# Turning attention probabilities by two row halves of the matrix engine, in a fused hybrid decoder layer

## The chip, the cores and the metric

The kernel runs on one core of one Trainium2 chip. The metric is the device time of one execution in microseconds, as the median of several runs. A core has a matrix engine (PE, whose weight loads the profile lists as PEld), a vector engine (DVE), an activation engine (ACT), a general engine (POOL) and an engine that issues most transfers (SP). They run their own instruction queues in order and meet at semaphores. PE writes into eight PSUM banks of 128 partitions by 512 floats; DVE and ACT copy from there.

## The reference

One decoder layer over 1024 tokens of width 1024. After an RMS norm, one input projection feeds two mixers: four heads of gated DeltaNet and eight heads of dilated sliding-window attention. Their outputs go through one output projection and a residual; a gated MLP with a short convolution and a final norm follow. The part that matters here is the attention: three branches, (window, dilation) of (128, 1), (512, 4) and (2048, 16), joined by their softmax denominators:

```python
for window, dil in DIL_PATTERNS:
    ...
    num, den, m = band_attention(stride(qf), stride(kf), stride(vf), window // dil)
...
out = num_tot / den_tot[..., None]
```

## The kernel before

All work is in one program, `hybrid_layer`. A planner written in the kernel (`Weave`) holds streams of work as generators. Each stream yields the time for which it has to wait by the planner's own costs; the planner then lets the stream with the lowest level run that is due. So PE's instruction order is a weave: the attention stream (level 5) goes when it is due, and between its steps stand the products of the dense projection (level 9) or the output projection (level 8). A dense column is two banks ("hf") of 24 full products each, three for each of eight slices of the input (high and low parts, `mm3`), 512 columns wide. PE's order is stamped and kept; the order on DVE and ACT is chosen by a scheduler, with the operations called through `uv` and `ua` preferred.

The attention works on four head pairs (pi), in each on eight blocks of 128 queries (n), two blocks at a time. A block's two heads (e) lie in partitions 0 to 63 and 64 to 127. In a block the three branches become one softmax over 128 or 256 local keys and up to 192 far keys of the same class mod 4 (`far`), with masks that hold the logarithm of how often a key is counted. The steps for a pair of blocks, each on lines named in the code below:

- `scores` (L900): products of q and k on PE's row halves, into two banks "asc" for the first block and two "atr" for the second. `normalise` (L932) makes probabilities `sm` (queries on partitions, both heads side by side) with DVE, ACT, DVE.
- `turn` (L964): PE turns `sm` so that keys lie on partitions. For each block and head, 128x128 transposes by the identity (`tp`, L192) fill one bank: first the local keys (one or two transposes), then the far ones (up to two). In all 184. `turned` (L945) copies the local part to `pt` with DVE and each far part to `pb` with ACT (L957 to L959).
- `values` (L979) multiplies `pt` with the values, on column halves of the array, one for each head. After four blocks, `merge_classes` (L988) does the same for `pb` ("class products"), and `give` (L1002) copies the result `oT` out of the bank with DVE.

`advance` (L1017) sets the order: turn the pair before, then the scores of the next pair, then the values of the pair before. `turn` yields ahead of each of its four banks, so dense products come between the first block's transposes and the second's. `TSLACK` (L39) shifts these due times.

At the end of the stage three other streams meet the attention. The gates (`gate`, L470: `zz` on ACT and DVE, then `og`) finish the DeltaNet heads. `mixer_splits` (L1067) splits the mixers' outputs into `ohi` and `olo`. `out_proj` (L1095) begins once the last group of blocks has started; its weights `whi` and `wlo` are made by ACT and DVE. The last copy of `turned` is an anchor there: the first low weights, and the slow gate and split operations, are ordered after it (L948 to L955). The scaled copy `xr` (L525) empties the dense banks that the output projection takes over.

Of the kernel before, what the change touches and what calls it, by code (L numbers as in the profile page):

```python
# [9 lines left out]
AF = mybir.ActivationFunctionType  # L10
# [5 lines left out]
P = 128  # L16
# [16 lines left out]
TOKEN = "pe"  # L33
# [5 lines left out]
TSLACK = -1.0, -0.6  # L39
# [105 lines left out]
def hybrid_layer(tc, I, out):  # L145
    nc = tc.nc
    wv = Weave()
# [3 lines left out]
    uv = Engine(wv, nc.vector, "vector", 0.07, 0.00105, first=tc.high_priority)  # L151
    ua = Engine(wv, nc.scalar, "scalar", 0.12, 0.00085, first=tc.high_priority)
    po_ = Engine(wv, nc.gpsimd, "gpsimd", 0.15, 0.0021)
# [9 lines left out]
    def tile_(pool, shape, dt, name, tag, bufs):  # L163
        return wv.slot(pool.tile(list(shape), dt, name=name, tag=tag, bufs=bufs), tag, bufs)
# [3 lines left out]
    def A(name, tag, dt=F32, shape=(P, 1024)):  # L168
        if tag in TURNS:
            i = turns[tag] = turns.get(tag, -1) + 1  # L170
            tag = TURNS[tag][i % len(TURNS[tag])]
        return tile_(lp, shape, dt, name, tag, SLOTS[tag])
# [4 lines left out]
    def const(name, shape, src=None):  # L177
        t = cp.tile(list(shape), F32, name=name)
        if src is not None:
            sy.dma_start(t, src)  # L180
        return t
# [3 lines left out]
    def after(inst, anchor, reason="keeps a slot free until it is needed"):  # L185
        tc.add_manual_dep(inst.ins, anchor.ins.name, order, reason=reason)
# [5 lines left out]
    def tp(dst, src):  # L192
        tc.stamp_issue_order_token(nc.tensor.transpose(dst, src, ident).ins, TOKEN)  # L193
        wv.product(0.11, dst, src)

    def mm3(dst, lhs, rhs, first, last, **kw):
        us = 0.2135 * rhs[0].shape[-1] / 512
        mm(dst, lhs[0], rhs[0], us, first, False, **kw)
        mm(dst, lhs[0], rhs[1], us, False, False, **kw)
        mm(dst, lhs[1], rhs[0], us, False, last, **kw)  # L200
# [23 lines left out]
    n1 = const("n1", [P, KT], I["n1"])  # L224
# [20 lines left out]
    def bank(tag, name="ps"):  # L245
        return tile_(pp_, (P, 512), F32, name, tag, 2)
# [7 lines left out]
    def half(i):  # L254
        return slice(i * 512, i * 512 + 512)
# [63 lines left out]
    ident = const("ident", [P, P], I["ident"])  # L319
# [565 lines left out]
    HALVES = (slice(0, 64), slice(64, 128))  # L885
# [3 lines left out]
    def attention():  # L889
# [52 lines left out]
                div = uv.tensor_scalar(sm[:, e, :wd], sm[:, e, :wd], den[:, e:e + 1], None, op0=OP.mult)  # L942
            return exp, div

        def turned(it, e, pt, pp):  # L945
            n1_ = it["n1"]
            inst = uv.tensor_copy(pt[:, :n1_], pp[:, :n1_])
            if it["g"]["pi"] == 3 and it["n"] == 7 and e == 1:  # L948

                lows = last.get("wlo", [])  # L950
                last["probabilities"] = inst
                for lo in lows:
                    after(lo, inst, "the probabilities go first")
                for slow in last["og"] + last.get("olo", [])[1:]:
                    after(slow, (lows or [inst])[0], "the first weights go first")  # L955

            for b, n_ in enumerate(far_blocks(it)):  # L957
                o = n1_ + b * P
                ua.activation(it["pb"][e][:32 * n_, it["u"], b], pp[:32 * n_, o:o + P], AF.Copy)  # L959

        def far_blocks(it):
            return [min(4, it["far"] // 32 - 4 * b) for b in range(-(-it["far"] // P))]

        def turn(pair):  # L964
            pts = A("pt", "dv*", shape=(P, 4, 256))
            for b, (it, tag) in enumerate(zip(pair, ("asc", "atr"))):
                sm, far, n1_ = it["sm"], it["far"], it["n1"]
                starts = [far + i for i in range(0, n1_, P)] + list(range(0, far, P))
                it["pt"] = []
                for e in range(2):  # L970
                    pt = pts[:, 2 * b + e, :]
                    it["pt"].append(pt)
                    pp = bank(tag)
                    yield wv.need(pp, sm, slack=TSLACK[b])
                    for i, o in enumerate(starts):
                        tp(pp[:, i * P:(i + 1) * P], sm[:, e, o:o + P])
                    turned(it, e, pt, pp)

        def values(pair):  # L979
            yield wv.need(pair[0]["po"], *pair[0]["pt"], slack=-PSLACK)  # L980
# [7 lines left out]
        def merge_classes(g):  # L988
            vcv = g["vc"].rearrange("p (c b d) -> p c b d", c=4, b=2)
            po, nb = g["po"], g["nb"]  # L990
            yield wv.need(*g["pb"], slack=-PSLACK)
            for c in range(4):
                for b in range(nb):

                    us = slice(2 if b == nb - 1 else 0, 4)
                    for e in range(2):
                        er = slice(64 * e, 64 * e + 64)
                        mm(po[er].rearrange("p (u t) -> p u t", u=4)[:, us, 32 * c:32 * c + 32],
                           vcv[:, c, b, er], g["pb"][e][:, us, b, 32 * c:32 * c + 32], 0.14 if us.start == 0 else 0.08,
                           False, c == 3 and b == nb - 1, skip_group_check=True)  # L1000

        def give(g):  # L1002
# [29 lines left out]
        for pi in range(4):  # L1032
            q, k, vn, vc = cur
            for hh in range(2):
                nb = 1 + hh
                if hh == 1 and pi < 3:
                    yield from wv.until(("a", pi + 1, 2))
                    qkv = att_load(pi + 1)
                po = bank("ch")
                pb = [A("pb", "qa", shape=(P, 4, nb, P)) for _ in range(2)]  # L1040
                for t in pb:
                    po_.memset(t[:, 2:, nb - 1], 0.0)
                    if nb > 1:
                        po_.memset(t[64:, 0, 0], 0.0)
                if pi == 3 and hh == 1:
                    wv.done.add("last group")
                g = dict(po=po, pb=pb, nb=nb, hh=hh, pi=pi, vc=vc)
                for u in (0, 2):
                    more = att_values(qkv[2]) if (hh, u) == (1, 2) and pi < 3 else None
                    yield from advance([dict(n=4 * hh + i, u=i, q=q, k=k, vn=vn, far=32 * max(4 * hh + i - 1, 0), po=po, pb=pb, g=g)  # L1050
                                        for i in (u, u + 1)], more)
            if pi < 3:
                cur = qkv[:2] + last["values"]
# [5 lines left out]
    last = {}  # L1059
# [35 lines left out]
    def out_proj():  # L1095
        yield from wv.until("dense")
        ws = [wk(I["wo"][m]) for m in MORDER[:2]]
        last["wlo"] = lows_made[-2:]
        yield from wv.until("last group")
        yield from wv.until("residual")  # L1100
        pts, third = {}, []
        todo = [(k, j) for k in range(8) for j in range(2)]
        while todo:

            now = [a for a in todo if ("ot", a[0]) in wv.done and (a[1] == 0 or "attention" in wv.done)]
            if not now:
                yield 0.3
                continue
            k, j = now[0]
            todo.remove(now[0])  # L1110
            m, w = MORDER[j], ws[j]
            if k == H and not third:

                third.extend(A(nm, "qa", F32R) for nm in ("whi", "wlo"))
                split(raw_weight(I["wo"][MORDER[2]]), *third)
            if m not in pts:
                pts[m] = [bank(("hf", "ch")[j]) for _ in range(2)]
            for h in range(2):
                yield wv.need(pts[m][h], *w, *ots[k])
                mm3(pts[m][h], [t[:, k, :] for t in w], [t[:, half(h)] for t in ots[k]], k == 0, k == 7)  # L1120
        for j, m in enumerate(MORDER):
            w = ws.pop(0)
            for h in range(2):
                if j > 1:
                    pt = bank("hf")
                    yield wv.need(pt, *w)
                    for k in range(8):
                        mm3(pt, [t[:, k, :] for t in w], [t[:, half(h)] for t in ots[k]], k == 0, k == 7)
                        yield 0.0
                else:  # L1130
                    pt = pts[m][h]
                ve.tensor_tensor(x1[m][:, half(h)], x1[m][:, half(h)], pt, op=OP.add)
            if j + 2 < 8:
                ws.append(wk(I["wo"][MORDER[j + 2]]) if j else
                          [t.rearrange("p (k m) -> p k m", k=KT) for t in third])
                load_residual(MORDER[j + 2])
            elif j == 6:
                up_first()
                wv.done.add("last weights")
            residual(m)  # L1140
        wv.done.add("proj")
# [577 lines left out]
```

## Time and profile before

| | |
|---|---|
| Median of 3 runs | 1214.62 us (1214.49 to 1215.29) |
| The profiled execution | 1213.62 us |
| Its span, first to last instruction | 1211.8 us |
| PE, DVE, ACT busy | 1197.8, 957.0, 575.2 us |
| The stretch 309 to 470 us (attention among dense products): PE, DVE, ACT busy | 161.00, 109.38, 66.91 us |
| Granted clock of PE | 0.998 |

A row of the timeline has the start in us, the length of the row, the engine, the line, the operation, what it writes and reads, the shape, and how many instructions of that kind follow one another. In square brackets stands idle time ahead of it and what ended that. Line 189 is the helper of all matmuls, 193 that of the transposes, 139 and 141 those of DVE, ACT and POOL, so the names of the tiles tell what an instruction is: `ps<-ident,sm` a transpose of probabilities, `ps<-kT,qT` scores, `ps<-pt,vn` values, `ps<-pb,vc` class products, `ps<-xhi,whi` and its two sisters the dense products, `ps<-ohi,whi` those of the output projection. A group's row ends with the busy time, the mean length of one in ns, and idle time just ahead.

### The profile page before, as it was taken

What the parts mean: (1) busy time and instruction counts of PE and PEld (TensorE: products, weight loads), DVE (VectorE), ACT (ScalarE), POOL (GpSimd) and SP (SyncE); (2) the same over time, 40 slices, a digit from 0 to 9 for tenths busy, and PEclk for the clock granted to TensorE, in tenths of its full rate; (3) what the DMA queues carried; (4) which work ended last, traced back from release to release, by engine and by line L of the source; (5) the groups of instructions that cost most, each with busy time, mean ns of one, the idle gap of its engine ahead of it and who ended that gap; (6) DMA issues with size and microseconds to landing.
All of it is one profiled execution on the core that took longest, in us unless ns stands there. A gap on an engine that the chain in (4) does not pass through costs nothing.

```text
span 1211.8 us, 18029 instructions
## 1 busy us (share of the span) xinstructions
PE 1197.8 (99%) x6878; PEld 993.0 (82%) x6878; DVE 957.0 (79%) x1531; ACT 575.2 (47%) x1128; POOL 53.9 (4%) x58
## 2 busy tenths in 40 slices
PE   9999999999999999999999999999999999999997
PEld 6888887898778787888888888888888888888886
DVE  7686985474666677667888989889898889898987
ACT  7383344364444444555544445444454454445451
POOL 0211110022000000000000000000000000000000
PEclk9999999999999999999999999999999999999999
DMA  7323236326532323434223132231322296356734
GB/s 233 107 74 101 71 123 170 108 78 209 165 119 92 113 63 95 173 125 157 68 72 105 53 104 76 81 105 53 105 68 89 92 373 220 114 180 224 235 101 147
DMA packets 81703, 152.70 MB, mean 126 GB/s; under 512 B 21552, under 2 KB 32592, under 8 KB 81616
## 3 DMA queue, kind: packets, MB, share of 16 engines
q1 hardware_dynamic: 81616, 151.55, 38.6%
q8 instruction: 54, 0.88, 0.3%
q14 instruction: 33, 0.27, 0.1%
HBM read 113.49 MB, written 35.93 MB: 123 GB/s over the span
## 4 chain that ended last, share of the span: by engine, by line
PE 90%; DVE 4%; ACT 2%; DMA 2%; issue 1%; POOL 0%; SPq 0%; POOLq 0%; DVEq 0%; ACTq 0%
PE ps L189 44%; PE pa L189 19%; PE dw L189 14%; PE pc L189 10%; PE ps L193 3%; DVE x1h L139 1%; DVE pr L139 1%; ACT sq L139 1%; ACT xhi L139 1%; DVE rstdB L139 0%; DMA wst<-in_wi 0%; DMA wst<-in_wu 0%; DMA xt<-in_xT 0%; POOL rs L139 0%; DMA wst<-in_wo 0%
## 5 line engine op out<-in xcount | busy, mean ns | idle before, releaser
L189 PE MATMUL dw<-pr 128*128 128x512 f32 (+1 forms) x984 | 211.4, 376 | 0.0
L189 PEld LDWEIGHTS dw<-pr 128*128 128x128 f32 x984 | 176.7, 188 | 33.6
L189 PE MATMUL ps<-xhi,whi 128*128 128x512 f32 x448 | 186.9, 417 | 0.0
L189 PE MATMUL ps<-xhi,wlo 128*128 128x512 f32 x448 | 175.7, 392 | 0.8 <-DVE wlo L139 0.8
L189 PE MATMUL ps<-xlo,whi 128*128 128x512 f32 x448 | 175.0, 391 | 0.1
L189 PE MATMUL pa<-T,pair 128*128 128x512 f32 x528 | 127.0, 389 | 0.0
L189 PEld LDWEIGHTS pa<-T,pair 128*128 128x128 f32 x528 | 99.0, 188 | 20.4
L189 PEld LDWEIGHTS ps<-xhi,wlo 128*128 128x128 f32 x448 | 84.1, 188 | 19.7 <-DVE wlo L139 1.2
L189 PEld LDWEIGHTS ps<-xhi,whi 128*128 128x128 f32 x448 | 84.3, 188 | 16.8 <-issue 2.7
L189 PEld LDWEIGHTS ps<-xlo,whi 128*128 128x128 f32 x448 | 84.6, 189 | 13.7 <-DVE xlo L139 0.5
L139 ACT ACTIVATE u<-pa 128x512 f32<-128x512 f32 x44 | 26.3, 599 | 110.7 <-PE pa L189 110.7
L139 DVE SCALAR_TENSOR_TENSOR y<-xu,fcw,y 128x1023 f32<-128x1023 f32 (+1 forms) x44 | 56.4, 1281 | 25.7 <-ACT y L139 25.6
L139 ACT ACTIVATE pr<-wd 128x1024 fp32r<-128x1024 f32 x33 | 35.0, 1061 | 76.2 <-DVE wd L139 43.2
L139 ACT ACTIVATE whi<-wst 128x1024 fp32r<-128x1024 f32 (+2 forms) x38 | 38.5, 1013 | 61.9 <-PE ps L189 54.8
L189 PE MATMUL pa<-B,A 128*128 128x512 f32 x264 | 63.4, 389 | 0.0
L189 PE MATMUL pc<-B,pair 128*128 128x512 f32 x264 | 63.4, 389 | 0.0
L189 PE MATMUL pc<-T,S 128*128 128x512 f32 x264 | 63.4, 389 | 0.0
L189 PE MATMUL pa<-T,S 128*128 128x512 f32 x264 | 63.4, 389 | 0.0
L139 DVE TENSOR_TENSOR wst<-wst 128x512 f32<-128x512 f32 x88 | 60.5, 687 | 0.8
L189 PE MATMUL ps<-B,pair 128*128 128x512 f32 x252 | 60.5, 389 | 0.0
L141 ACT ACTIVATE sm<-sm,mx 128x128 f32<-128x128 f32 (+7 forms) x64 | 35.4, 555 | 51.7 <-DVE mx L141 51.7
L189 PEld LDWEIGHTS pc<-T,S 128*128 128x128 f32 x264 | 49.6, 188 | 10.3
(235 smaller groups left out, 2271.6 us busy)
## 6 DMA issues: line engine op xcount, KB each, us to landing
wst<-in_wu SPq DMA_DIRECT2D x44, 512.0 KB, 3.8
wd<-in_wd SPq DMA_DIRECT2D x44, 512.0 KB, 4.4
wst<-in_wi SPq DMA_DIRECT2D x25, 512.0 KB, 3.7
upark<-y SPq DMA_DIRECT2D x22, 512.0 KB, 3.7
r<-upark SPq DMA_DIRECT2D x22, 512.0 KB, 9.9
apark<-aqkv SPq DMA_DIRECT2D x12, 512.0 KB, 3.0
wa<-in_wd SPq DMA_DIRECT2D x22, 256.0 KB, 3.0
wst<-in_wo SPq DMA_DIRECT2D x8, 512.0 KB, 3.8
```

The costliest lines, as they stand in the source:

```text
L139: return getattr(eng, op)(*a, **kw)
L141: return getattr(eng, op)(*a, **kw)
L189: tc.stamp_issue_order_token(nc.tensor.matmul(dst, lhs, rhs, start=start, stop=stop, **kw).ins, TOKEN)
L193: tc.stamp_issue_order_token(nc.tensor.transpose(dst, src, ident).ins, TOKEN)
```

## The change

A transpose of 128 queries by 128 keys becomes two, each of 64 queries on one row half of the array (`tp_half`). The first queries' halves of both heads go to one bank, the last queries' halves to the other. `turn` waits once, for the first block's probabilities and all four banks, and then issues both blocks without a yield. `turned` copies a query half of both heads at once. `pb` is made by far block with both heads in it, instead of by head with all far blocks; the zero fills and the class products follow. The ordering after the last copy is left out where the output projection's products have begun.

```diff
+    def tp_half(dst, src, rows):
+        tc.stamp_issue_order_token(nc.tensor.transpose(dst, src[rows], ident[rows, rows]).ins, TOKEN)
+        wv.product(0.033, dst, src)
...
-        def turned(it, e, pt, pp):
-            n1_ = it["n1"]
-            inst = uv.tensor_copy(pt[:, :n1_], pp[:, :n1_])
-            if it["g"]["pi"] == 3 and it["n"] == 7 and e == 1:
+        def turned(it, h, pts, b, pp):
+            nl = it["n1"] // P
+            th = slice(64 * h, 64 * h + 64)
+            inst = uv.tensor_copy(pts[:, 2 * b:2 * b + 2, :it["n1"]].rearrange("p e (i t) -> p e i t", t=P)[:, :, :, th],
+                                  pp[:, :, :nl, :])
+            if it["g"]["pi"] == 3 and it["n"] == 7 and h == 1:
                 lows = last.get("wlo", [])
                 last["probabilities"] = inst
-                for lo in lows:
+                for lo in [] if "products" in last else lows:
...
-                for slow in last["og"] + last.get("olo", [])[1:]:
+                for slow in [] if "products" in last else last["og"] + last.get("olo", [])[1:]:
...
-            for b, n_ in enumerate(far_blocks(it)):
-                o = n1_ + b * P
-                ua.activation(it["pb"][e][:32 * n_, it["u"], b], pp[:32 * n_, o:o + P], AF.Copy)
+            for i, n_ in enumerate(far_blocks(it)):
+                ua.activation(it["pb"][i][:32 * n_, it["u"], :, th], pp[:32 * n_, :, nl + i, :], AF.Copy)
...
         def turn(pair):
+            def wait():
+                return max(wv.need(pair[0]["sm"]) + TSLACK[0], *[wv.slot_free(t, n) for t in ("asc", "atr")
+                                                                 for n in (1, 2)])
+            while wait() > 1e-3:
+                yield wait()
             pts = A("pt", "dv*", shape=(P, 4, 256))
             for b, (it, tag) in enumerate(zip(pair, ("asc", "atr"))):
...
+                pps = [bank(tag)[:, :2 * len(starts) * 64].rearrange("p (e i t) -> p e i t", e=2, t=64) for _ in range(2)]
                 for e in range(2):
-                    pt = pts[:, 2 * b + e, :]
-                    it["pt"].append(pt)
-                    pp = bank(tag)
-                    yield wv.need(pp, sm, slack=TSLACK[b])
                     for i, o in enumerate(starts):
-                        tp(pp[:, i * P:(i + 1) * P], sm[:, e, o:o + P])
-                    turned(it, e, pt, pp)
+                        for pp, rows in zip(pps, HALVES):
+                            tp_half(pp[:, e, i, :], it["sm"][:, e, o:o + P], rows)
+                for h in range(2):
+                    turned(it, h, pts, b, pps[h])
...
-                           vcv[:, c, b, er], g["pb"][e][:, us, b, 32 * c:32 * c + 32], 0.14 if us.start == 0 else 0.08,
+                           vcv[:, c, b, er], g["pb"][b][:, us, e, 32 * c:32 * c + 32], 0.14 if us.start == 0 else 0.08,
...
-                pb = [A("pb", "qa", shape=(P, 4, nb, P)) for _ in range(2)]
-                for t in pb:
-                    po_.memset(t[:, 2:, nb - 1], 0.0)
-                    if nb > 1:
-                        po_.memset(t[64:, 0, 0], 0.0)
+                pb = [A("pb", "qa", shape=(P, 4, 2, P)) for _ in range(nb)]
+                po_.memset(pb[-1][:, 2:], 0.0)
+                if nb > 1:
+                    po_.memset(pb[0][64:, 0], 0.0)
...
             m, w = MORDER[j], ws[j]
+            last["products"] = True
```

In the changed kernel the line of `tp_half` is L198.

More of the change, by code (lines that the diff above doesn't have):

```diff
@@ L964, in turn @@
         def turn(pair):
+            def wait():
[3 more added lines that the diff above has]
+                yield wait()
             pts = A("pt", "dv*", shape=(P, 4, 256))
             for b, (it, tag) in enumerate(zip(pair, ("asc", "atr"))):
-                sm, far, n1_ = it["sm"], it["far"], it["n1"]
-                starts = [far + i for i in range(0, n1_, P)] + list(range(0, far, P))
-                it["pt"] = []
+                it["pt"] = [pts[:, 2 * b + e, :] for e in range(2)]
+                starts = [it["far"] + i for i in range(0, it["n1"], P)] + list(range(0, it["far"], P))
+                pps = [bank(tag)[:, :2 * len(starts) * 64].rearrange("p (e i t) -> p e i t", e=2, t=64) for _ in range(2)]
                 for e in range(2):
-                    pt = pts[:, 2 * b + e, :]
-                    it["pt"].append(pt)
-                    pp = bank(tag)
-                    yield wv.need(pp, sm, slack=TSLACK[b])
                     for i, o in enumerate(starts):
-                        tp(pp[:, i * P:(i + 1) * P], sm[:, e, o:o + P])
-                    turned(it, e, pt, pp)
+                        for pp, rows in zip(pps, HALVES):
+                            tp_half(pp[:, e, i, :], it["sm"][:, e, o:o + P], rows)
+                for h in range(2):
+                    turned(it, h, pts, b, pps[h])
         def values(pair):
```

## The prediction

> **What bounds the kernel now.** I read the page first: busy time, then the chain that ended last.
>
> ```profile
> PE 1197.8 (99%) x6878; PEld 993.0 (82%) x6878; DVE 957.0 (79%) x1531; ACT 575.2 (47%) x1128; POOL 53.9 (4%) x58
> ...
> PE 90%; DVE 4%; ACT 2%; DMA 2%; issue 1%; POOL 0%; SPq 0%; POOLq 0%; DVEq 0%; ACTq 0%
> ```
>
> The matrix engine carries the chain. Busy time of pipelined matmuls overlaps, so I next took the table by stretches, from the first scores to the last class product, and in it the groups by form: matmuls, then weight loads.
>
> ```profile
> 309.00:470.00 161.00, 161.00 (x1542) 128.21 (x1541) 109.38 (x323) 66.91 (x210) 5.04 (x18) 1.00 0.32 101
> ```
> ```profile
> L193 PE MATMUL ps<-ident,sm 128*128 128x128 f32 x184 | 25.4, 273 | 0.0
> ...
> L189 PE MATMUL ps<-pb,vc 128*64 128x64 f32 x128 | 7.1, 221 | 0.0
> ```
> ```profile
> L193 PEld LDWEIGHTS ps<-ident,sm 128*128 128x128 f32 x184 | 21.8, 140 | 4.0
> L189 PEld LDWEIGHTS ps<-pt,vn 128*64 128x64 f32 x240 | 12.8, 136 | 3.7 <-issue 3.0 <-DVE pt L141 0.4
> L189 PEld LDWEIGHTS ps<-kT,qT 64*128 64x128 f32 x128 | 10.5, 186 | 6.3 <-issue 3.2 <-ACT pb L141 1.8 <-DVE pt L141 0.4
> ```
>
> In 161 us PE is never idle (0.0 ahead of every matmul group), DVE works 109 and ACT 67. So time is what PE's instructions take one after another, plus any wait put into its order. The 184 transposes are the change's subject. Prices come from the timeline of PE: in a row of n matmuls, (row length less one matmul) / (n - 1) is the pace.
>
> ```profile
> 327.43 1.09 PE L189 MATMUL ps<-pt,vn 128*64 128x128 f32 x16
> 328.36 0.63 PE L189 MATMUL ps<-pb,vc 128*64 128x64 f32 x16
> ```
> ```profile
> 345.31 1.03 PE L193 MATMUL ps<-ident,sm 128*128 128x128 f32 x8
> 346.10 0.48 PE L189 MATMUL ps<-xhi,whi 128*128 128x512 f32 x1
> 346.42 0.39 PE L189 MATMUL ps<-xlo,whi 128*128 128x512 f32 x1
> ```
>
> A full transpose: (1.03 - 0.273)/7 = **0.108 us**. Where two halves of the array work at once (here column halves), a 128-wide matmul paces at (1.09 - 0.279)/15 = 0.054, a 64-wide one at (0.63 - 0.221)/15 = **0.0273**. The weights of a transpose load quickly: 140 ns a load, like 64 columns (136), against 186 for 128 columns of the scores' row halves.
>
> **The change part by part.**
>
> *Transposes.* 184 full ones go, 184 x 0.108 = 19.9 us. 368 halves come, each 64 rows by 128 columns of weights, 64 columns moving. No such row exists. Bounds: 0.0273 each if the two row halves overlap as the column halves do (368 x 0.0273 = 10.0), 0.054 if they do not (19.9). I take 0.0273: it is the row with the same moving width, and the scores below show that row halves overlap. Gain **9.8**.
>
> *Mode changes.* Full transposes stand among full products without a gap: after eight, ending at 346.34, the next product ends at 346.58, 0.24 later, against 0.23 from one product to the next. Halves do not:
>
> ```profile
> 309.02 0.39 PE L189 MATMUL ps<-xhi,wlo 128*128 128x512 f32 x1
> 309.34 0.93 PE L189 MATMUL ps<-kT,qT 64*128 64x128 f32 x8
> 310.20 0.50 PE L189 MATMUL ps<-xhi,whi 128*128 128x512 f32 x1
> ```
> ```profile
> 351.00 1.51 PE L189 MATMUL ps<-pb,vc 128*64 128x128 f32 x32
> 352.44 0.44 PE L193 MATMUL ps<-ident,sm 128*128 128x128 f32 x2
> ```
>
> The scores are eight matmuls on row halves; four 128-wide and four 256-wide at the paired pace are 4 x 0.054 + 4 x 0.108 = 0.65. From the end of the product before (309.41) to theirs (310.27) is 0.86: 0.2 to get in, with the slow weight load. The next product ends 0.43 later (310.70): **0.20 to get out**. Changing mode into quick-loading transposes took 0.37 (352.51 to 352.88) less two transposes, **0.15**. In the built order of the changed kernel the 16 turns each end in full products; 13 follow full products, three the class products, where a mode change is paid already. Cost 16 x 0.20 + 13 x 0.15 = **5.2**; at 0.2 in, 5.8.
>
> The Trainium skill, TensorEngine Tiling (Array Packing), Key Properties, speaks against this change: changing the tiling mode drains the engine. It gives no price; the rows above agree and give it. Without that rule the sum would be 5.2 us better.
>
> *Second block's wait.* A turn now issues both blocks when the first is due. Before, 0.65 us or more of products and the first block's transposes lay between. In most turns that is hidden: in the one quoted below, the second block's probabilities are done at 425.63 and the halves want them at 425.50 + 0.15 + 16 x 0.0273 = 426.1. Not where blocks 0 and 1 follow the class products at once (three turns):
>
> ```profile
> 352.71 0.66 DVE L141 TENSOR_SCALAR sm<-sm,mx 128x256 f32<-128x256 f32 x2
> ```
>
> They are done at 353.37; the halves want them near 352.7. Up to 0.6 each; one DVE scaling ahead of this softmax moves behind it, so I take 0.3: **0.9** in all, bounds 0 and 1.8. Behind the wait stand all of PE's products, so it is paid in full.
>
> *Copies out of the banks.* Same count, same elements (DVE 128x256, ACT 128 per row), so nothing for themselves. But nine products now stand between the last transpose and the next scores, which need the four banks; before, six after the second block. Where DVE has other work first, PE waits. The dearest place is the turn of blocks 6 and 7 of head pair 2, where the built order now has a gate (zz on ACT, zz and og on DVE) ahead of the copies:
>
> ```profile
> 424.81 0.82 DVE L141 TENSOR_SCALAR sm<-sm,mx 128x448 f32<-128x448 f32 x2
> ...
> 425.50 1.04 PE L193 MATMUL ps<-ident,sm 128*128 128x128 f32 x8
> 426.13 0.86 DVE L141 COPY pt<-ps 128x256 f32<-128x256 f32 x2 [0.51 <-PE ps L193]
> ...
> 428.16 0.87 ACT L141 ACTIVATE pb<-ps 128x128 f32<-128x128 f32 x4 [0.71 <-DVE pt L141]
> ```
> ```profile
> 433.25 1.22 DVE L139 SCALAR_TENSOR_TENSOR zz<-zz,xr 128x1024 f32<-128x1024 f32 x1
> ...
> 435.69 1.21 DVE L139 TENSOR_TENSOR og<-og,zz 128x1024 f32<-128x1024 f32 x1
> ```
>
> DVE would be at zz from 425.7, at the copies from 428.1 and done with four (0.43 each) at 429.8; ACT's last two copies, 0.22 each, end at 430.25. PE turns from 425.50, 0.15 + 32 x 0.0273 = 1.0, then 0.20 + 9 x 0.23: ready at 428.85. Wait **1.4**. At three other turns with a split or gate ahead the same count gives about 0.2 each: together **2.0**, bounds 0.2 and 3.5.
>
> *The end of the stage.* Before, PE waits for a bank at the start of the output projection:
>
> ```profile
> 470.22 1.23 DVE L139 TENSOR_TENSOR wlo<-wst,whi 128x1024 fp32r<-128x1024 f32 x1 [1.78 <-ACT whi L139]
> 471.37 1.22 DVE L139 SCALAR_TENSOR_TENSOR zz<-zz,xr 128x1024 f32<-128x1024 f32 x1
> 472.50 1.09 DVE L139 COPY oT<-ps 128x512 f32<-128x512 f32 x1
> 473.42 1.23 DVE L139 TENSOR_TENSOR og<-og,zz 128x1024 f32<-128x1024 f32 x1
> 474.56 0.69 DVE L139 TENSOR_TENSOR xr<-ps,rstdB 128x512 f32<-128x512 f32 x1
> 475.15 3.49 DVE L139 TENSOR_TENSOR olo<-og,ohi 128x1024 fp32r<-128x1024 f32 x3
> 478.55 0.69 DVE L139 TENSOR_TENSOR xr<-ps,rstdB 128x512 f32<-128x512 f32 x1
> ```
> ```profile
> 477.23 0.39 PE L189 MATMUL ps<-ohi,wlo 128*128 128x512 f32 x1
> 479.30 0.50 PE L189 MATMUL ps<-ohi,whi 128*128 128x512 f32 x1 [1.68 <-DVE xr L139]
> ```
>
> From 477.62 to 479.80 less one product: 1.95 lost, because DVE reaches the last xr late. In the changed order 39 products, not 30, stand between the class products' end (T) and the projection, and zz and oT go before wlo. DVE then takes, by the steps from start to start, oT 0.92, wlo 1.15, og 1.14, xr 0.59, olo 3.40 from T + 0.2: free at T + 7.4, while the last product ends at T + 9.2. Only xr itself is left to wait for, about 0.3. Gain **1.65**, bounds 0 and 1.95. What is late next is the fourth head's gate; it hangs on the same xr as before, so it keeps its distance.
>
> The zero fills of pb (24 become 12, twice as large) lie on POOL, 5.0 us busy in 161; nothing waits for them. SP's queue keeps its order and count.
>
> **Sum:** -9.8 + 5.2 + 0.9 + 2.0 - 1.65 = -3.35. The profiled execution took 1213.62 us (span 1211.8), 1.0 under the median of the runs, 1214.62. So 1210.3 for it, and **1211.2** for the median.
>
> **The rivals.**
>
> *Waits eat it.* The 1.65 at the end does not come, and the scores wait 3.5 instead of 2.0: -3.35 + 3.15 = -0.2, 1214.4. For it: those places rest on an order and no trace. Against: PE had slack at most of them.
>
> *No new waits.* 2.9 less: -6.25, 1208.4. For it: PE shows no wait of this kind now. Against: the gate ahead of the copies, counted above, gives 1.4 by itself.
>
> *Weights bound the halves (slower).* Each half still loads 128 columns. If row-half loads are the scores' (186 ns, as full as 128 moving columns, 0.108 a pair) the pair costs that: 184 x 0.108 = 19.9, no gain, and the mode changes stay: -3.35 + 9.8 = +6.45, 1221.1. It decides where a pair costs over 0.073 (19.9 less 6.45, over 184). Against: transposes load in 140 ns.
>
> *It does not overlap.* The halves run one after another, or a 64-wide one is no cheaper: 368 x 0.054, again 1221.1. Against: the scores' 0.65 at paired pace, and 0.0273 at 64 wide.
>
> The Trainium skill, TensorEngine Tiling, Instruction Overhead, has about 60 cycles under every matmul; an estimate by that page at its 2.4 GHz is 25 ns, so 64 columns would just escape. The trace agrees: 27 ns.
>
> **How the numbers follow.** Forecast 0.55, own range 1209.0 to 1213.5 (a half at 0.0273 to 0.033, waits 1.2 to 4); waits eat it 0.19; no new waits 0.13; weights bound 0.08; no overlap 0.05. A measurement can tell about 0.2%, 2.4 us. Faster by that: nearly nine tenths of the forecast and all of "no new waits", 0.61. Slower: the last two and a rest, 0.14. The same: 0.25. The range leaves out the slower 0.13 and the edges: 1207.6 to 1215.2.
>
> **What would show it.** L198: 368 matmuls, 64 rows, rows of 32 lasting about 1.07 us; the next product ending 0.43 after them; scores after blocks 6 and 7 of pair 2 waiting on pb or pt over 1 us; the gap before the second bank of the projection near 0.3. A row of 32 near 1.9 us proves the forecast wrong, and so do waits ahead of scores summing over 4 us.

## The result and the profile after

The changed kernel takes **1210.96 us** (median of 20 runs, 1209.82 to 1214.62), the kernel before 1215.00 beside it (20 runs, 1213.3 to 1217.86). The ratio is **0.9971**, 95% interval 0.9965 to 0.9978: 4.0 us between the medians, 2.7 to 4.3 by the interval. The forecast was 1211.2. The sum came out close, but not its terms.

The page of the changed kernel, busy time and the chain by engine:

```profile
PE 1197.0 (99%) x7062; PEld 988.1 (82%) x7062; DVE 957.1 (79%) x1531; ACT 573.5 (47%) x1128; POOL 53.9 (4%) x46
...
PE 91%; DVE 4%; ACT 2%; issue 1%; DMA 1%; POOL 0%; SPq 0%; POOLq 0%; DVEq 0%; ACTq 0%
```

184 instructions more on PE (7062 for 6878), and PE carries the chain as before. The profiled execution of the changed kernel took 1213.97 us, one of its longest: near 206 us, long before any changed instruction, PE stood for some 2 us and then ran at half pace for about 3 (granted clock 0.64 from 209 to 212 us). So I compare only the stage, from the end of the first head pair's `ident,vT` transposes to the end of the output projection's last product: 258.63 us before, 254.14 after, **4.49 less**.

Next the groups by form in the stretch 309 to 470 us, matmuls and weight loads:

```profile
L198 PE MATMUL ps<-ident,sm 64*128 64x64 f32 x368 | 15.4, 228 | 0.2
```
```profile
L198 PEld LDWEIGHTS ps<-ident,sm 64*128 64x128 f32 x368 | 13.0, 138 | 5.2 <-issue 4.2 <-DVE sm L141 0.8
L189 PEld LDWEIGHTS ps<-kT,qT 64*128 64x128 f32 x128 | 10.6, 186 | 6.2 <-issue 3.2 <-ACT pb L141 2.5
```

All 368 halves are there, and their weights load in 138 ns. Two things are new: 0.8 us of waits for `sm` ahead of halves, and 2.5 instead of 1.8 for `pb` ahead of scores. All idle time ahead of the scores' loads together is the same, 6.2 for 6.3.

From the timeline of PE one turn of 32 halves, and then the turns of blocks 0 and 1 of the second and the last head pair:

```profile
347.43 0.39 PE L189 MATMUL ps<-xhi,wlo 128*128 128x512 f32 x1
347.75 1.21 PE L198 MATMUL ps<-ident,sm 64*128 64x64 f32 x32
348.89 0.50 PE L189 MATMUL ps<-xhi,whi 128*128 128x512 f32 x1
...
354.37 0.96 PE L198 MATMUL ps<-ident,sm 64*128 64x64 f32 x12
...
434.84 0.59 PE L198 MATMUL ps<-ident,sm 64*128 64x64 f32 x12
```

The 32 halves take 1.21 us, a pace of (1.21 - 0.228)/31 = 0.0317, not 0.0273. The product behind them ends at 349.39, 0.43 after the halves' end (348.96), as forecast. Of the two rows of 12 one holds a wait: 0.96 against 0.59.

Added up over the stage, each kind of work from the end of what came before it to its own end (dense and projection products: what goes beyond 0.2265 each, their pace in a long row), in us. The output projection's first long run of products is the "last run":

| | before | after | difference | forecast |
|---|---|---|---|---|
| turns (`ident,sm`) | 20.54 | 14.51 | -6.03 | -9.8 + 13 x 0.15 + 0.9 = -6.95 |
| products between, over their pace | 4.06 | 6.81 | +2.75 | 16 x 0.20 = +3.2 |
| scores of the local keys (128 weight columns) | 16.38 | 16.42 | +0.04 | +2.0 |
| last run of products, over its pace | 2.29 | 1.03 | -1.26 | -1.65 |
| scores of the far keys (32 weight columns), values, class products, `vT` | 31.90 | 31.89 | 0.0 | 0 |

The rest of the program gives a part back. After the output projection both kernels make a norm, for which PE waits on POOL; here with ACT's first step behind the weights' transfer and the transfer's issue, first before, then after:

```profile
582.14 1.09 PE L193 MATMUL ps<-ident,rs 128*128 128x128 f32 x8 [0.78 <-POOL rs L139]
...
571.58 0.63 ACT L139 ACTIVATE A<-wst 128x512 fp32r<-128x512 f32 x1 [2.19 <-DMA wst<-in_wu]
...
565.77 1.08 SPq L139 DMA_DIRECT2D wst<-in_wu  x2
```
```profile
582.18 1.09 PE L193 MATMUL ps<-ident,rs 128*128 128x128 f32 x8 [1.80 <-POOL rs L139]
...
571.61 0.63 ACT L139 ACTIVATE A<-wst 128x512 fp32r<-128x512 f32 x1 [3.21 <-DMA wst<-in_wu]
...
564.78 1.08 SPq L139 DMA_DIRECT2D wst<-in_wu  x2
```

The transfers are issued 0.99 us earlier, and yet ACT starts on their data at the same time, 6.8 us after the issue instead of 5.8; PE waits 1.80 instead of 0.78. So about 3.5 of the 4.5 us reach the end, as the ratio has it (0.0029 x 1215 = 3.5). All traces with halves show this wait at 1.66 to 1.99 us; of the three experiments with full transposes throughout two show 0.68 and 0.90, near the kernel before, and one 1.92 (`before_bank_first` below). Whether the change causes it stays open.

### The profile page after: what moved, and what is told of

Read it like the earlier page. It is cut to its first block, busy times and chain, and to the rows that moved or that the text cites. A ratio compares the mean times of both kernels' runs of the same rounds, so it can differ in the third digit from the quotient of the medians.

```text
span 1212.2 us, 18348 instructions
## 1 busy us (share of the span) xinstructions
PE 1197.0 (99%) x7062; PEld 988.1 (82%) x7062; DVE 957.1 (79%) x1531; ACT 573.5 (47%) x1128; POOL 53.9 (4%) x46
## 4 chain that ended last, share of the span: by engine, by line
PE 91%; DVE 4%; ACT 2%; issue 1%; DMA 1%; POOL 0%; SPq 0%; POOLq 0%; DVEq 0%; ACTq 0%
PE ps L189 45%; PE pa L189 19%; PE dw L189 14%; PE pc L189 10%; PE ps L193 2%; DVE x1h L139 1%; PE ps L198 1%; DVE pr L139 1%; ACT sq L139 1%; ACT xhi L139 1%; DMA wst<-in_wu 0%; DVE rstdB L139 0%; DMA wst<-in_wi 0%; DMA xt<-in_xT 0%; POOL rs L139 0%
## 5 line engine op out<-in xcount | busy, mean ns | idle before, releaser
L189 PEld LDWEIGHTS pc<-B,pair 128*128 128x128 f32 x264 | 49.5, 188 | 10.3
```

Source lines behind the costliest of these rows:

```text
L189: tc.stamp_issue_order_token(nc.tensor.matmul(dst, lhs, rhs, start=start, stop=stop, **kw).ins, TOKEN)
```

## The experiments

Theory A is the forecast's: halves overlap and are cheap, each passage into and out of the row-half mode costs 0.15 and 0.20, and waits are what the order makes late. Each ratio is to the kernel before.

**The wait taken out again, each block turned when it is due.**

```diff
-            while wait() > 1e-3:
-                yield wait()
...
+                yield wv.need(*pps, it["sm"], slack=TSLACK[b])
```

> The changed kernel, but each block's halves are issued when that block's probabilities and its two banks are due, with products between the blocks as before. Theory A (PE's own time: the overlap of the halves gains some 8.4 us, each passage into and out of the row mode costs 0.14 + 0.205): 16 more passages, +5.5, and the waits on the second block's probabilities (0.75) go: about 0.8 us slower than before (ratio 1.0007), 4.8 slower than the changed kernel. Theory B (the gain is the new order with one wait for both blocks, the end of the stage above all; passages hide behind something): no more than 1.5 us slower than the changed kernel, ratio 0.998.

Measured: 1.0074 (1.0060 to 1.0087), 1224.26 us, stage 266.32: 12.2 more than the changed kernel, where A had 4.8 and B at most 1.5 in the whole time. Both miss. PE's timeline, the turn of blocks 2 and 3 of the last head pair, a wait for scores two turns on, and the first block of the last turn:

```profile
459.43 0.59 PE L198 MATMUL ps<-ident,sm 64*128 64x64 f32 x12 [0.76 <-DVE sm L141]
459.95 0.50 PE L189 MATMUL ps<-xhi,whi 128*128 128x512 f32 x1
...
461.01 0.61 PE L198 MATMUL ps<-ident,sm 64*128 64x64 f32 x12
...
474.54 0.97 PE L189 MATMUL ps<-kT,qT 64*128 64x256 f32 x4 [1.32 <-ACT pb L141]
...
482.39 0.71 PE L198 MATMUL ps<-ident,sm 64*128 64x64 f32 x16 [2.50 <-DVE sm L141]
```

The halves now come in shorter rows (12 here, for 24) with products between. Products go 3.6 us further over their pace, 16 exits more (0.22 each); the turns take 5.2 more: 16 x 0.13 = 2.1 are entries by the changed kernel's price, 3.6 are new waits for `sm`, nearly all of it the two shown, and the 0.75 of waits for the second block's probabilities behind the class products (measured further down) is gone, as A had it; scores wait 2.7 more, the last run 0.7. The passages, 5.7 in all, are near the prices on record (16 x 0.35 = 5.6). The other 6.5 are waits, in balance, that neither theory had. PE's order is now another, and what ends the waits shown is DVE and ACT; why they come later was not followed further. So joining the blocks saves passages, but this run doesn't price that alone.

**Full transposes, both blocks at once.** The kernel before with the changed kernel's wait ahead of a turn, no yield between blocks, and its condition on the ordering at the end.

```diff
-                for lo in lows:
+                for lo in [] if "products" in last else lows:
...
-                for slow in last["og"] + last.get("olo", [])[1:]:
+                for slow in [] if "products" in last else last["og"] + last.get("olo", [])[1:]:
...
+            while wait() > 1e-3:
+                yield wait()
...
-                    yield wv.need(pp, sm, slack=TSLACK[b])
...
+            last["products"] = True
```

> The kernel before, full 128x128 transposes, but both blocks of a turn issued at once after one wait. Theory A: the transposes cost what they did, no passages are added; the wait for the output projection's second bank shrinks from 2 to about 0.3-0.7 us (-1.2), the second block's probabilities and the copies are waited for up to 1 us in all: -0.5 us against before, ratio 0.9996. Theory B: as the changed kernel, -4 us, ratio 0.997.

Measured: 1.0003 (0.9994 to 1.0012), stage 258.82. B falls: waiting once and issuing both blocks at once wins nothing by itself. Waits of PE's weight loads from 311 to 482 us, in this kernel and in the kernel before (total us, times, longest):

```profile
PEld ps L189 <- DVE pt L141: 1.8, 5, 0.4
PEld ps L189 <- ACT pb L141: 1.7, 4, 0.6
PEld ps L189 <- DVE xr L139: 1.2, 1, 1.2
PEld ps L193 <- ACT pb L141: 0.6, 1, 0.6
```
```profile
PEld ps L189 <- DVE xr L139: 2.5, 2, 2.1
PEld ps L189 <- ACT pb L141: 1.8, 5, 0.4
PEld ps L189 <- DVE pt L141: 0.7, 2, 0.4
```

The wait for `xr` falls from 2.1 to 1.2, less than A's 0.3 to 0.7, and the last run goes 1.36 over its pace: of the 1.26 gained there by the changed kernel, 0.93 come with the order, without halves. As much is lost to new waits for `pt` (0.7 to 1.8) and, ahead of transposes, for `pb` (0.6): scores take 0.8 us more in the stage, turns 0.3, the `vT` transposes 0.4. So the gain needs the halves. Not all of it lies in PE's time for them: from this kernel to the changed one the turns take 6.3 less and the products behind them 3.0 more, 3.3 in balance; the other 1.4 are waits (scores 0.7, `vT` 0.4, the last run 0.3). The two wait by the same rule, but PE's built order is not quite the same (372 products between, for 387), nor are the copies' layouts, so those 1.4 are not put down to one cause.

**Rows of the array one after the other.** The changed kernel, in each block all halves of rows 0 to 63 first.

```diff
-                for e in range(2):
-                    for i, o in enumerate(starts):
-                        for pp, rows in zip(pps, HALVES):
+                for pp, rows in zip(pps, HALVES):
+                    for e in range(2):
+                        for i, o in enumerate(starts):
```

> The changed kernel, but in each block all halves of rows 0-63 are issued first, then all of rows 64-127, so that neighbours in PE's order stand on the same rows. Same instructions, banks and copies. Theory A (the gain is overlap of the two row halves, which needs neighbours on different rows): a half paces at about 0.054 instead of 0.031, 368 x 0.023 = +8.5 us against the changed kernel, +4.5 against before, ratio 1.0037. If the halves are cheap by themselves (64 columns moving) and not by overlap: as the changed kernel, ratio 0.997.

Measured: 0.9998 (0.9984 to 1.0013), stage 259.07; between the two. The turn that took 1.21 us takes

```profile
345.67 1.62 PE L198 MATMUL ps<-ident,sm 64*128 64x64 f32 x32
```

0.045 a half. The single starts in the trace say why. In the changed kernel they lie 3 and 59 ns apart in turn: two halves start together, a pair every 62 to 63 ns. Here a half follows another on the same rows after 62 ns, so a half by itself costs **0.062**, not 0.054; but from about the third on, halves of the other rows start among them, 6 and 55 ns apart, although the program has them later. The semaphore marks show it: of 24 halves, those that end a bank stand 6th, 12th, 18th and 24th in the program, but 9th, 14th, 21st and 24th by start, in seven of the eight turns of 24. The overlap is what makes the change pay: with a part of it gone, the turns take 3.7 us more, scores wait 1.0 more, and the gain is gone. One thing this run can't part: within a block each row half writes a bank of its own, so halves that follow one another on the same rows also follow one another into the same bank.

**Each half twice.** The planner's price of one is halved with it, so that PE's order stays.

```diff
-        wv.product(0.033, dst, src)
+        wv.product(0.0165, dst, src)
...
-                        for pp, rows in zip(pps, HALVES):
+                        for pp, rows in 2 * list(zip(pps, HALVES)):
```

> As the changed kernel, with every transpose of a half issued twice into the same place: 736 halves instead of 368, alternating between the two row halves as before, nothing else moved on PE. Theory A (a half costs what the rows of 24 and 32 in the changed kernel's trace show, 0.0313 us, also where many follow one another): 368 x 0.0313 = 11.5 us over the changed kernel, about 1222.5, ratio to the kernel before 1.0066. Rival B (the pace of my prediction, 0.0273, holds and the rows show something that comes once in a row): 10.0 us, 1221.0, ratio 1.0053. Rival C (part of the halves' time lies in waits that are there anyway, such as the second block's probabilities): less than 9 us, ratio under 1.0045. In the trace, the length of a row of 64 tells A from B: 0.23 + 63 x 0.0313 = 2.2 us or 1.95 us, if the first gap is the same.

Measured: 1.0068 (1.0056 to 1.0081), 1223.27 us; 12.1 more in the stage. Two rows:

```profile
331.92 1.72 PE L198 MATMUL ps<-ident,sm 64*128 64x64 f32 x48
...
345.93 2.22 PE L198 MATMUL ps<-ident,sm 64*128 64x64 f32 x64
```

A row of 48 takes 1.72 and one of 64 takes 2.22: 0.50/16 = 0.0313 a half; with 1.21 for 32, (2.22 - 1.21)/32 = 0.0316. A is right, and B and C fall: the price is one of each half, not of a row, and nearly all of it is paid. The first gap comes once: 1.142 from the product before to the end of 32 halves, less 32 x 0.0316, is 0.13 to get in. 1.1 of the 12.1 are class products that now wait for `pb`.

**Blocks 0 and 1 as before**, by full transposes in two steps, all others by halves.

```diff
+            if pair[0]["n"] == 0:
+                yield from turn_first(pair)
+                return
```

> The changed kernel, but the four turns of blocks 0 and 1 are done as before: full transposes, two steps, copies by head. Theory A: there the halves gain 0.65 - 0.38 = 0.27 and pay 0.34 for the passage, and PE waits 0.4 on the second block's probabilities at two of them: doing those as before is 0.5 us better than the changed kernel, ratio 0.9967; in the trace no wait on sm is left. Theory B: slower than the changed kernel by a share of the gain (a quarter of the turns, 1 us), ratio 0.998.

Measured: 0.9965 (0.9953 to 0.9978), stage 254.85, 0.7 more than the changed kernel, where A had 0.5 less. The waits for `sm` are gone, products go 0.6 less over their pace, but at the output projection the second bank is late again:

```profile
477.51 0.50 PE L189 MATMUL ps<-ohi,whi 128*128 128x512 f32 x1 [1.57 <-DVE xr L139]
```

The last run of products is 2.20 over its pace (changed kernel 1.03). Two small things changed places; by the times alone the kernels can't be told apart.

**The end of the stage by itself.** Five kernels order DVE's second and third low part (`olo`) later. Three do so after the second scaled copy `xr`: the kernel before, the changed kernel and the one above, each with this edit.

```diff
-                ve.tensor_tensor(t[:, sl], pair[h], rstdB[:, sl], op=OP.mult)
+                last["xr"] = ve.tensor_tensor(t[:, sl], pair[h], rstdB[:, sl], op=OP.mult)
...
+                if i in (1, 2):
+                    after(lo, last["xr"], "the last bank is emptied first")
```

> The kernel before, with the second and third low part of the mixers (olo) ordered on DVE after the scaled copy xr that empties the second dense bank; nothing of the turns is changed and PE's order is the same. Theory A (the wait of 1.95 us at the start of the output projection is DVE's order alone, and the gain that the change shows there needs no halves): the wait falls to about 0.35, 1.6 us less, ratio to the kernel before 0.9987. Rival B (the low parts that were put off are then late for the next products, or the last gate is): no gain, ratio 1.000 or above.

> The changed kernel with the same order on DVE (two low parts after the second scaled copy). Theory A (in the changed kernel DVE already waits 0.40 us for PE ahead of that copy, so the order gives nothing more): the same as the changed kernel within 0.3 us, ratio to the kernel before 0.997. Rival B (the low parts put off are late for the second bank's products): up to 1 us slower than the changed kernel, 0.998.

> Blocks 0 and 1 turned as before the change, by full transposes in two steps, all others by halves, and with the two low parts after the second scaled copy. Theory A (turning blocks 0 and 1 in two steps saves the 0.75 us of waits on the second block's probabilities, and was no gain by itself only since the wait of 2.0 us at the start of the output projection came back): that wait falls to about 0.4, 1.2 to 1.6 us less than with the low parts first; near 1209.9, ratio to the kernel before 0.9955, 0.7 to 1.2 us ahead of the changed kernel. Rival B (the end of the stage is set by something else, the last gate or the weights): no difference from the changed kernel, 0.9967.

Measured: 1.0001 (0.9993 to 1.0010), 0.9974 (0.9959 to 0.9990) and 0.9964 (0.9952 to 0.9977). In the three, the last run is 1.84, 1.86 and 1.85 over its pace, whatever it was before (2.29, 1.03, 2.20). From `before_bank_first`, DVE and then PE:

```profile
477.81 0.69 DVE L139 TENSOR_TENSOR xr<-ps,rstdB 128x512 f32<-128x512 f32 x1 [0.95 <-PE ps L189]
478.42 1.22 DVE L139 TENSOR_TENSOR olo<-og,ohi 128x1024 fp32r<-128x1024 f32 x1
479.55 1.22 DVE L139 TENSOR_TENSOR wlo<-wst,whi 128x1024 fp32r<-128x1024 f32 x1
```
```profile
478.56 0.50 PE L189 MATMUL ps<-ohi,whi 128*128 128x512 f32 x1
...
480.82 0.50 PE L189 MATMUL ps<-ohi,wlo 128*128 128x512 f32 x1 [0.84 <-DVE wlo L139]
```

`xr` now waits for PE, as it should, and the wait for the bank is gone. But a low part slipped ahead of `wlo`, and PE waits 0.84 for that: a wait took the place of a wait, which none of my expectations had. In the changed kernel it made the end worse. Hence two more, the kernel before and the one with blocks 0 and 1 in full, with a line more:

```diff
+                    after(lo, last["wlo"][-1], "the second weights go first")
```

> The kernel before, with the second and third low part (olo) ordered on DVE after the second scaled copy xr and also after the second low weights wlo. With xr alone ahead of them, the wait for the second bank went (1.68 to near nothing), and a wait of 0.84 for wlo, which had slipped behind a low part, came in its place. Theory A (both waits are DVE's order): the first run of products of the output projection takes 1.0 to 1.2 us over its pace instead of 2.29 (the kernel before) and 1.84 (xr alone first); 1.1 to 1.3 us less in the stage, ratio to the kernel before near 0.999. Rival B (the second weights' high part on ACT, which waits for PE, sets the start): still 1.8, ratio 1.000.

> Blocks 0 and 1 turned by full transposes in two steps, all others by halves, with the low parts after xr and wlo. Theory A: the first run of products takes 1.0 to 1.2 us over its pace (1.85 with xr alone first), so the stage is 253.6 us, 0.5 to 0.8 under the changed kernel's 254.1, and no other wait comes; ratio to the kernel before 0.9957, too near the changed kernel's 0.9971 for the times alone to part them. Rival B (ACT's high part of the second weights sets the start): stage 254.4 as with xr alone first, 0.9964.

Measured: 0.9994 (0.9984 to 1.0004) and 0.9968 (0.9957 to 0.9979); the last run 1.30 and 1.36 over its pace, stages 257.64 and 253.97. In the kernel before, 1.0 us of the end's wait goes by DVE's order alone, just short of A's 1.1 to 1.3; this rests on the stage, since the interval of the ratio holds both A's 0.999 and B's 1.000. With halves and blocks 0 and 1 in full, the stage is 0.17 shorter than the changed kernel's, less than A's 0.5 to 0.8, since 0.3 more is left at the end. No version is faster than the changed kernel by an amount that can be measured.

## Why the prediction came out right, point by point

*Transposes: forecast -9.8, measured 19.9 - 368 x 0.0315 = **-8.3**.* The term that was mis-sized. The mechanism holds: row halves overlap, `halves_by_rows` takes a part of that away and loses the gain. The size came from `ps<-pb,vc`, 0.0273, as "the row with the same moving width"; that row loads 64 weight columns, a half loads 128. What sets 63 ns for a pair was not separated. A floor under each matmul, as in the prediction's estimate of 25 ns (the page named there gives no clock), does not set it: two halves on different rows start 3 ns apart, and two on the same rows 62.

*Mode changes: forecast +5.2, measured **+4.5**.* Out: products behind halves end 0.21 to 0.24 late, 3.62 in 16 places. The sum took full transposes to leave without a gap; the 32 exits before cost 0.80 in all, 0.025 each, so the net is 2.8 instead of 3.2. In: 0.13 instead of 0.15, 1.7 for 13. The rule that I set against the change, that switching the tiling mode drains the engine (the Trainium skill, TensorEngine Tiling (Array Packing), Key Properties), fits the 0.22 and 0.13 a passage; that it is a drain that takes this time, no run here shows.

*Second block's wait: forecast +0.9, measured **+0.75**.* At two of the three places, 0.89 and 0.89 from the class products' end to the halves' end, against 0.52 at the third: 0.375 each where 0.3 was taken. DVE's last scaling at the first and at the third place:

```profile
354.17 0.77 DVE L141 TENSOR_SCALAR sm<-sm,mx 128x256 f32<-128x256 f32 x2
...
434.40 0.62 DVE L141 TENSOR_SCALAR sm<-sm,mx 128x256 f32<-128x256 f32 x2
```

It ends 0.57 behind the halves' start (354.94 against 354.37) where PE waits, and 0.18 (435.02 against 434.84) where it doesn't. `halves_twice` confirms that it is a wait: there the same place, with 24 halves, takes 1.02, only 0.13 more.

*Copies out of the banks: forecast +2.0, measured **+0.2**.* The step that failed. (The scores' sum, +0.04, also holds a wait of 0.2 for `xr` that is gone.) The place forecast at 1.4, blocks 6 and 7 of head pair 2, on PE, DVE and ACT:

```profile
427.99 1.21 PE L198 MATMUL ps<-ident,sm 64*128 64x64 f32 x32
...
431.39 1.16 PE L189 MATMUL ps<-kT,qT 64*128 64x128 f32 x8
```
```profile
426.77 0.82 DVE L141 TENSOR_SCALAR sm<-sm,mx 128x448 f32<-128x448 f32 x2
427.52 1.23 DVE L139 SCALAR_TENSOR_TENSOR zz<-zz,xr 128x1024 f32<-128x1024 f32 x1
428.78 1.23 DVE L139 TENSOR_TENSOR og<-og,zz 128x1024 f32<-128x1024 f32 x1
429.92 1.41 DVE L141 COPY pt<-ps 128x256 f32<-128x256 f32 x4
```
```profile
430.37 1.43 ACT L141 ACTIVATE pb<-ps 128x128 f32<-128x128 f32 x8 [2.89 <-DVE pt L141]
```

The order is the forecast's: probabilities, `zz`, `og`, then four copies. But the probabilities are done at 427.59, 0.4 ahead of the halves; I had laid the old times under the new order, where they were done 0.13 behind the transposes' start. And copies in a row go every 0.33 us ((1.41 - 0.42)/3), not 0.43, the length of one. ACT ends at 431.80, 3.81 behind the halves' start, where the forecast had 4.75. The scores then take 0.23 longer than elsewhere (1.085 from the product before, against 0.856). At the three other places there was no wait.

*The end of the stage: forecast -1.65, measured **-1.26**.* PE and DVE:

```profile
477.52 0.39 PE L189 MATMUL ps<-ohi,wlo 128*128 128x512 f32 x1
478.01 0.50 PE L189 MATMUL ps<-ohi,whi 128*128 128x512 f32 x1
...
479.05 0.39 PE L189 MATMUL ps<-olo,whi 128*128 128x512 f32 x1
479.46 0.50 PE L189 MATMUL ps<-ohi,wlo 128*128 128x512 f32 x1
```
```profile
473.37 3.50 DVE L139 TENSOR_TENSOR olo<-og,ohi 128x1024 fp32r<-128x1024 f32 x3 [0.30 <-ACT ohi L139]
477.27 0.69 DVE L139 TENSOR_TENSOR xr<-ps,rstdB 128x512 f32<-128x512 f32 x1 [0.40 <-PE ps L189]
```

DVE waits for PE ahead of `xr`, as forecast, and the second bank's first product ends 0.60 after the one before, 0.37 more than one product (0.3 forecast). What came besides is 0.3 at 479.46, counted the same way (0.52 from end to end, less one product): `wlo` is late. The step's "what is late next" named the gate; it was the weights, and the kernels of the last experiment pay up to 0.84 for the same thing.

*The rivals.* "Waits eat it" and "no new waits" lie on either side: 0.95 of new waits came, of 2.9. "Weights bound the halves" falls at its price, since they load in 138 ns, not 186, and a pair costs 0.063, short of the 0.073 at which the change would lose; whether the weights make the difference between 0.0546 and 0.063 a pair stays open. "It does not overlap" falls by the pairs' starts. The sum was -3.35, the stage gave -4.5. The gains were taken 1.9 too large (halves 1.5, the end 0.4), the losses 2.8 too large (waits 2.1, counting the wait for `xr` that is gone, and passages 0.7); the 0.2 left is in the rows of full transposes, at 0.109 each rather than 0.108. The waits, 0.95, lie below the 1.2 with which the forecast's own range began, and its sign of over 1 us ahead of the scores behind blocks 6 and 7 did not come. Then a later transfer took about 1 us back, of which nothing was forecast. So the direction and the overlap were foreseen, but that the total came within 0.3 us of the measured one is luck: errors of 1 to 3 us cancelled.

## What to carry to other kernels

Price a packed instruction from a row with the same weights and the same moving columns where there is one (here a row with half the weight columns gave 0.0273 for 0.0315), and count the passages in and out: here 0.13 and 0.22 us a turn took 4.5 of 8.3 us, so a turn has to be long, and joining two blocks in one turn makes it so. When a wait is forecast from a new order, move the other engines' times with it, and take a run of equal copies by its pace, not by one copy's length. And before an ordering is put on an engine, ask what is pushed behind: the wait for a bank here turned into a wait for weights.

## What was not expected of the hardware

Transposes on the two row halves of the array do not keep the program's order among themselves: with all of one row half first, the other's start from about 0.18 us on among them (9th, 14th, 21st and 24th by start instead of 6th, 12th, 18th and 24th). The start of this document has every engine run its queue in order; between the row halves PE does not. Leaving the mode costs the full products 0.22 us, entering it 0.13 where the weights load in 138 ns, against 0.2 for scores with 186 ns. And a transfer of weights issued 0.99 us earlier let ACT start no earlier, 6.8 instead of 5.8 us after its issue, in the one execution of each kernel that was profiled; the cause is open.
